# Attention blocks of a two-layer decoder trunk: 1/z, V and value transfers on other DMA queues, one down-projection look-ahead

## The chip, the core and the metric

The kernel runs on one core of a Trainium2 chip. A core has TensorE (PE, matrix products; its weight loads are listed as PEld), VectorE (DVE), ScalarE (ACT), GpSimd (POOL) and SyncE (SP), which run instruction streams of their own and meet at semaphores. A DMA is issued by SP, ACT or POOL and carried out by 16 shared DMA engines. SP's and ACT's queues appear as hardware queues in the profile, POOL's as a software queue. The metric is the device time of one execution in microseconds (us). Each engine works through its own list in order, so an instruction that waits holds everything behind it on that engine, DMA issues included.

## The reference

The model has one short convolution layer, one attention layer, and a SwiGLU feed-forward after each. Sequence 1024, width 1024, 16 heads of 64, all in float32. What matters here is the attention layer: three dilated branches per head, each a banded causal window, combined by their own log-denominators, which makes one softmax over the union of the branches' keys.

```python
BRANCHES = ((128, 1), (512, 4), (2048, 16))

def dilated_attention_mixer(h, w_qkv, w_out, rel_bias):
    bsz, seq, _ = h.shape
    qkv = (h @ w_qkv).reshape(bsz, seq, 3, N_HEADS, HEAD_DIM)
    q, k, v = qkv[:, :, 0], qkv[:, :, 1], qkv[:, :, 2]
    outs, lses = [], []
    for window, dilation in BRANCHES:
        o, l = dilated_branch(q, k, v, rel_bias, window, dilation)
        outs.append(o)
        lses.append(l)
    alpha = jax.nn.softmax(jnp.stack(lses, axis=0), axis=0)
    o = jnp.sum(alpha[..., None] * jnp.stack(outs, axis=0), axis=0)
    return o.reshape(bsz, seq, D_MODEL).astype(h.dtype) @ w_out

def swiglu(h, w_gate, w_up, w_down):
    return (jax.nn.silu(h @ w_gate) * (h @ w_up)) @ w_down
```

## The kernel before

Activations are kept with features on the 128 partitions and the 1024 positions along a row, in eight tiles `X[0..7]`. Matrix products split each operand into a high and a low part and use three matmuls for each product (L370 to L372, L561 to L563, L1501 to L1503); the splits are made by ACT (the high part, L142) and DVE (the low part, L143). Weights arrive through `load_raw` (SP, L156) and are split by `ensure`, in one fixed list `ops`; `take(key, ahead)` hands out the next one and makes sure that `ahead` further ones are already split. Buffers of 4 KB per partition come from one pool of 41 pages; a new tile takes a page over and waits for its last readers.

The schedule is written by hand: generators yield at points where other work may go between, and the order in which the Python code runs is the order of each engine's list.

The stages, in order: convolution mixer; feed-forward 0 with its last down-projection loop (`feed_forward`: one tile `n` of eight after another, each with `take(("d", 0, n))` and two 512-wide products); the Q/K phase (`qk.mix()`, Q and K of the first six head pairs); attention; feed-forward 1. After the last of feed-forward 0's down weights, the list `ops` goes on with the Q/K weights, so that looking ahead in the last down tiles splits Q/K weights early.

Attention is a loop over 16 heads, `slot(n, ...)`, here called block n, with one more at the end. Head pair p is n // 2, its half a is n % 2. A block interleaves on PE: the scores of head n (`scores`, L1556 and L1557), the value products of head n-1 (`values`, L1629), and dense filling work (V tiles by `value_tiles`, Q/K projections of the last two pairs, the output projection of the first half). What else a block issues:

- `load_bias(n+1)` (SP, L1452 and L1453) and `load_kq(n+1)` (SP, L1530 to L1534): bias, keys `ka`, queries `qa` and their low part `ql` of the next head. They come back from DRAM, where the projections left them. `classes(n+1)` copies the keys in another order into `kca` (ACT, L1540).
- `softmax(n)`: POOL takes the maximum over partitions (`mb`, L1610), DVE subtracts (L1618), ACT takes the exponential (L1619). The value products need the results.
- `load_values(p)`: the values of pair p into the single buffer `vx`, six DMAs per pair (ACT, L1518 and L1520), from `vdram`, where `value_tiles` stored them (ACT, L1510, four DMAs for each of eight tiles). Up to block `LAG` = 13 it is issued in the odd blocks, after the loads of head n+1; the last pair's comes at the end of block 14's first half. The last value product of the pair before must have read `vx`.
- `values` ends with ACT's copies of the products and the denominators to `o` and `z` (L1652, L1653).
- `finish(p)`: the denominators of a pair go to DRAM and back in another shape (POOL, L1661 and L1664), DVE takes 1/z (L1666), POOL stores it (L1667), and SP loads it spread over 128 partitions (L1669): 64 rows hold one head's 1024 numbers, the other 64 the other head's. One block later `attended()` multiplies (DVE, L1716) and POOL stores the result to `odram` (L1717). The last pair takes another way; its second half is spread by two POOL loads of 64 rows (L1707).
- Before block 12, `load_attended` (SP, L1804) fetches the first four results from `odram`; they are split (`w_hi<-oin`) for the output projection of the first half.

In the compiled order the DMAs of SP and ACT use eight completion semaphores in turn, those of POOL another eight.

Of the kernel before, what the change touches and what calls it, by code (L numbers as in the profile page):

```python
# [17 lines left out]
S = 1024  # L18
# [31 lines left out]
LAG = 13  # L50
# [48 lines left out]
def trunk(ctx: ExitStack, tc: tile.TileContext, x, gains_in, cwi, ck, cwo, wqkv, wo, relb,  # L99
          wg, wu, wd, oneh, ident, out):  # L100
    nc = tc.nc
# [69 lines left out]
    def take(key, ahead=1):  # L171
        i = op_state[1]
        assert ops[i][0] == key, (ops[i][0], key)
        ensure(i + ahead)
        op_state[1] += 1
        return made.pop(i)
# [210 lines left out]
    def both(w, ks, acts):  # L387
        banks = two_banks()
        run(product(w, ks, acts, banks))
        return banks  # L390
# [99 lines left out]
    def add_to_x(n, banks):  # L490
        for (c0, c1), b in banks.items():
            nc.vector.tensor_tensor(out=X[n][:, c0:c1], in0=X[n][:, c0:c1], in1=b[:, :c1 - c0], op=ALU.add)  # L492
# [733 lines left out]
    class Swiglu(Strassen):  # L1226
# [111 lines left out]
        def feed_forward(self, stats, last_step, after, final=None):  # L1338
            prep = []

            def start(n):
                if n == 0:
                    last_step()
                    for m in (6, 7):
                        combos[self.key, 1](m)
                    ensure(self.at(3, 1))
                if n == self.key + 1:
                    next(stats)
                    combos[self.key, 2](6)
                    ensure(self.at(0, 6))  # L1350
                elif n == self.key + 2:
                    run(stats)
                    prep.append(self.second_half())
                    next(prep[0])
                    nc.scalar.activation(scratch, eps, AF.Silu)
                    ensure(self.at(1, 6))
                elif n == 4:
                    ensure(self.at(1, 7))
                elif n in (5, 7, 8, 10, 12):
                    next(prep[0], None)  # L1360
                if n in (8, 24):
                    self.ahead = 3 if n == 8 else 2

            self.run(start)
            key = ("d", self.key)
            if final:
                final(key, self.plain, self.hid)
                return
            for n in range(KT):
                add_to_x(n, both(take(key + (n,)), self.plain, self.hid))  # L1370
                after(n)

    def by_columns(key, ks, acts, pieces, each, between, wide=4, ahead=1, added=lambda i, n: None):
# [92 lines left out]
    def attention(norm, qk):  # L1466
# [5 lines left out]
        vx = scope["pool"].tile([128, 16, 192], F32, name="vx", tag="vx", bufs=1)  # L1472
# [17 lines left out]
        def value_tiles(g, j):  # L1490

            if j == 0:
                wv[:] = [take(("v", g, i), 1) for i in range(2)]
            v = page("v")
            for b4 in range(4):
                t = 4 * j + b4
                b = bank()[:, :256]
                for k in range(KT):
                    (hi, lo), (whi, wlo) = qk.h[j][k], wv[k // 4]
                    a, c = slice(b4 * 128, b4 * 128 + 128), slice(k % 4 * 256, k % 4 * 256 + 256)  # L1500
                    nc.tensor.matmul(b, hi[:, a], whi[:, c], start=k == 0, stop=False)  # L1501
                    nc.tensor.matmul(b, hi[:, a], wlo[:, c], start=False, stop=False)
                    nc.tensor.matmul(b, lo[:, a], whi[:, c], start=False, stop=k == KT - 1)  # L1503
                    if k % 2:
                        yield
                nc.scalar.activation(v[:, b4 * 256:b4 * 256 + 256], b, AF.Identity, scale=norm.r[:, t:t + 1])
                yield
            vd = vdram[g]
            for r in range(4):
                nc.scalar.dma_start(bass.AP(vd.tensor, vd.offset + (512 * j + r) * 256,  # L1510
                                          [[16 * 256, 32], [4 * 256, 4], [1, 256]]), v[32 * r:32 * r + 32])

        def load_values(p):
            src = vdram[p // 2]
            for a in range(2):
                off = src.offset + p % 2 * 128 + a * 64
                dims = slice(128 * a, 128 * a + 64)
                nc.scalar.dma_start(vx[:, 0:8, dims], bass.AP(src.tensor, off, [[256, 128], [128 * 256, 8], [1, 64]]))  # L1518
                for h in range(2):
                    nc.scalar.dma_start(vx[:, 8 + 4 * h:12 + 4 * h, dims],  # L1520
                                        bass.AP(src.tensor, off + 512 * 256 * h, [[1024, 128], [256, 4], [1, 64]]))

        def load_kq(n):
# [132 lines left out]
        def finish(p):  # L1656

            o, z = OZ.pop(p)
            if p < NPAIR - 1:
                zd, rd = zdram[p]  # L1660
                nc.gpsimd.dma_start(zd, z[0:65:64])  # L1661
                yield
                zc = scope["pool"].tile([128, 16], F32, name="zc", tag="zc", bufs=2)
                nc.gpsimd.dma_start(zc, bass.AP(zd.tensor, zd.offset, [[16, 128], [1, 16]]))  # L1664
                yield
                nc.vector.reciprocal(zc, zc)  # L1666
                nc.gpsimd.dma_start(bass.AP(rd.tensor, rd.offset, [[16, 128], [1, 16]]), zc)  # L1667
                yield
                nc.sync.dma_start(z, bass.AP(rd.tensor, rd.offset, [[S, 2], [0, 64], [1, S]]))  # L1669
                yield  # L1670
                put_off.append((p, o, z))
                return

            zd, rd = zdram[p]
            wide = lambda t: bass.AP(t.tensor, t.offset, [[HALF, 2], [1, HALF]])
            thin = lambda t: bass.AP(t.tensor, t.offset, [[8, 128], [1, 8]])
            nc.gpsimd.dma_start(wide(zd), z[0:65:64, HALF:])
            zc = scope["pool"].tile([128, 8], F32, name="zl", tag="zl", bufs=1)
            nc.gpsimd.dma_start(zc, thin(zd))
            acts[p] = page("o_hi", F32R), page("o_lo", F32R)  # L1680

            def scaled(c0, c1):
                q = slice(c0, c1)
                nc.vector.tensor_tensor(out=o[:, q], in0=o[:, q], in1=z[:, q], op=ALU.mult)

            def parts(h):
                split(o[:, half(h)], [t[:, half(h)] for t in acts[p]])

            for c in (0, 256):
                nc.vector.reciprocal(z[:, c:c + 256], z[:, c:c + 256])  # L1690
                scaled(c, c + 256)
                if c:
                    parts(0)
                    nc.scalar.activation(scratch, eps, AF.Sqrt)
                yield

            def rest():
                scaled(HALF, S)
                parts(1)

            last_part.append(rest)
            yield
            ensure(ahead_ao + KT - AO_WIDE)
            nc.vector.reciprocal(zc, zc)
            nc.gpsimd.dma_start(thin(rd), zc)
            for a in range(2):
                nc.gpsimd.dma_start(z[64 * a:64 * a + 64, HALF:],  # L1707
                                    bass.AP(rd.tensor, rd.offset + a * HALF, [[0, 64], [1, HALF]]))
            ensure(ahead_ao + KT - AO_WIDE + 4)
            yield  # L1710
# [11 lines left out]
        def slot(n, dense, ndense, late=0, hook=iter(())):  # L1722
# [5 lines left out]
            p, a = divmod(n, 2)  # L1728
            if n < H:
                new = dict(bias=bias.pop(n))  # L1730
                sc = scores(p, a, new)
            else:
                sc = iter(())
            if n + 1 < H:
                bias[n + 1] = load_bias(n + 1)
                load_kq(n + 1)
# [14 lines left out]
                extra = finish(p - 1)  # L1751
            used = 0
            if lagged:
                if a:
                    load_values(p)
                for i in range(8):
                    next(sc, None)
                    if n or i % 2:
                        other(1)
                        used += 1  # L1760
                    if i in (0, 3):
                        next(extra, None)
                run(sc)
            else:
                if a == 0 and not late:
                    other(1)
                    used += 1
                for i in range(8):
                    next(sc, None)
                    next(pv, None)  # L1770
                    next(pv, None)
                    if i >= late and i % 2 == 0:
                        other(1)
                        used += 1
                run(sc)
                run(pv)
                if a == 0:
                    extra = finish(p - 1)
                if a == 0 and n < H:
                    load_values(p)  # L1780
# [279 lines left out]
```

## Time and profile before

| | us |
|---|---|
| median of 3 runs | 2200.01 (2198.01 to 2201.2) |
| profiled execution | 2200.59 |
| its span, first to last instruction | 2198.8 |
| mean granted TensorE clock | 0.986 |
| PE busy | 2121.2 |
| DVE busy | 1746.1 |
| ACT busy | 1006.7 |
| POOL busy | 228.5 |

The profile is one execution. Its head gives busy time per engine; a view by stretches gives the same for any window, with the clock that was granted to TensorE and the share of time in which the 16 DMA engines were busy. The view of waits has rows "who waited <- for whom: us in all, times, longest". The chain of waits follows back from the last instruction what released what. A timeline row is start, duration, engine, line, operation, tiles, and in brackets the idle time before it with its releaser. "SPq" and "ACTq" are the DMA issues of an engine.

### The profile page before, as it was taken

The numbers are of one execution on the slowest core, as the hardware profiler recorded it, in microseconds if no ns is written. First come the engines' busy times: TensorE is split into PE (matmuls) and PEld (weight loads), VectorE is DVE, ScalarE is ACT, GpSimd is POOL, SyncE is SP. The second block draws the span as 40 slices with busy tenths as digits, with TensorE's granted clock in tenths as the row PEclk, the third lists the DMA queues.
The fourth block names the chain that finished last, engine by engine and source line by source line (L and its number), as shares of the span: only waits on it lengthen the run. The fifth ranks groups of instructions, "written<-read, shape, count | busy, mean of one in ns | idle before, by whom it ended". The sixth has DMA issues, their size and how long they took to land. (4 is left out here: it accounts for less than half of the span.)

```text
span 2198.8 us, 30951 instructions
## 1 busy us (share of the span) xinstructions
PE 2121.2 (96%) x11086; PEld 1817.0 (83%) x11086; DVE 1746.1 (79%) x3272; ACT 1006.7 (46%) x1848; POOL 228.5 (10%) x324
## 2 busy tenths in 40 slices
PE   9999999999999999999998888799999999999998
PEld 7788888888888888877898778688888888888887
DVE  8898669988888888779856467567998888888886
ACT  7333336444444554355443443434644444446335
POOL 1000000101010010001312122121010100101000
PEclk9999999999999999999999999899999999999999
DMA  7222643233333584334674656755223333267532
GB/s 216 88 90 68 229 144 86 87 106 111 106 111 106 185 235 158 108 125 139 235 190 118 167 166 169 195 157 180 68 105 106 108 108 106 104 210 213 174 91 77
DMA packets 146215, 304.90 MB, mean 139 GB/s; under 512 B 48732, under 2 KB 59212, under 8 KB 146062
## 3 DMA queue, kind: packets, MB, share of 16 engines
q1 hardware_dynamic: 74862, 197.22, 29.4%
q0 software_dynamic: 25424, 78.42, 11.1%
q10 hardware_dynamic: 45776, 27.29, 4.3%
q8 instruction: 88, 1.44, 0.3%
q14 instruction: 65, 0.53, 0.1%
HBM read 212.48 MB, written 83.05 MB: 134 GB/s over the span
## 5 line engine op out<-in xcount | busy, mean ns | idle before, releaser
L563 PE MATMUL bank<-b,w 128*128 128x512 f32 x1952 | 760.9, 390 | 6.1 <-DVE w L143 6.0
L561 PE MATMUL bank<-b,w 128*128 128x512 f32 x1952 | 762.7, 391 | 1.5 <-ACT w L142 1.1
L562 PE MATMUL bank<-b,w 128*128 128x512 f32 x1952 | 760.4, 390 | 0.6 <-DVE b L872 0.6
L563 PEld LDWEIGHTS bank<-b,w 128*128 128x128 f32 x1952 | 366.4, 188 | 87.5 <-DVE w L143 10.8
L561 PEld LDWEIGHTS bank<-b,w 128*128 128x128 f32 x1952 | 366.6, 188 | 78.0 <-ACT w L142 1.7
L562 PEld LDWEIGHTS bank<-b,w 128*128 128x128 f32 x1952 | 366.6, 188 | 76.1 <-DVE b L872 1.4
L142 ACT ACTIVATE w<-combo 128x512 fp32r<-128x512 f32 (+2 forms) x488 | 249.1, 540 | 231.2 <-DVE combo L190 214.1
L143 DVE TENSOR_TENSOR w<-combo,w 128x512 fp32r<-128x512 f32 (+2 forms) x488 | 276.3, 579 | 38.1 <-ACT w L142 37.4
L567 ACT ACTIVATE part<-bank 128x512 f32<-128x512 f32 x186 | 110.7, 596 | 388.6 <-PE bank L563 386.7
L143 DVE TENSOR_TENSOR w<-raw,w 128x512 fp32r<-128x512 f32 (+2 forms) x342 | 188.5, 572 | 46.9 <-ACT w L142 46.9
L571 DVE TENSOR_TENSOR part<-part,bank 128x256 f32<-128x256 f32 (+1 forms) x366 | 170.6, 495 | 31.2 <-PE bank L563 16.7
L142 ACT ACTIVATE w<-raw 128x512 fp32r<-128x512 f32 (+2 forms) x342 | 167.1, 530 | 52.3 <-PE bank L563 12.2
L370 PE MATMUL bank<-w_hi,w 128*128 128x512 f32 (+1 forms) x400 | 153.9, 385 | 18.6 <-ACT w_hi L142 13.7
L371 PE MATMUL bank<-w_lo,w 128*128 128x512 f32 (+1 forms) x400 | 150.2, 375 | 1.6 <-DVE w_lo L143 1.6
L372 PE MATMUL bank<-w_hi,w 128*128 128x512 f32 (+1 forms) x400 | 149.9, 375 | 1.1 <-DVE w L143 1.1
L791 DVE TENSOR_TENSOR x<-x,bank 128x512 f32<-128x512 f32 x136 | 92.5, 680 | 29.3 <-PE bank L563 29.3
L190 DVE TENSOR_TENSOR combo<-raw 128x512 f32<-128x512 f32 (+1 forms) x172 | 111.2, 646 | 0.0
L492 DVE TENSOR_TENSOR x<-x,bank 128x512 f32<-128x512 f32 (+1 forms) x104 | 66.2, 642 | 54.9 <-PE bank L372 54.3
L370 PEld LDWEIGHTS bank<-w_hi,w 128*128 128x128 f32 x400 | 75.9, 190 | 32.4 <-ACT w_hi L142 14.1
L371 PEld LDWEIGHTS bank<-w_lo,w 128*128 128x128 f32 x400 | 76.0, 190 | 15.6 <-DVE w_lo L143 2.9
L372 PEld LDWEIGHTS bank<-w_hi,w 128*128 128x128 f32 x400 | 75.8, 190 | 15.4 <-DVE w L143 2.1
L554 DVE TENSOR_TENSOR b<-hin,b 128x512 fp32r<-128x512 f32 x126 | 79.4, 683 | 9.4 <-ACT b L553 9.3
(245 smaller groups left out, 3491.8 us busy)
## 6 DMA issues: line engine op xcount, KB each, us to landing
hin<-part SPq DMA_DIRECT2D x126, 256.0 KB
raw<-in_ffn_w_gate SPq DMA_DIRECT2D x44, 512.0 KB
raw<-in_ffn_w_up SPq DMA_DIRECT2D x44, 512.0 KB
part<-sum POOLq DMA_DIRECT2D x72, 256.0 KB, 2.3
raw<-in_ffn_w_down SPq DMA_DIRECT2D x48, 384.0 KB
raw<-in_attn_w_qkv SPq DMA_DIRECT2D x27, 512.0 KB
raw<-in_conv_w_in SPq DMA_DIRECT2D x24, 512.0 KB
part<-part POOLq DMA_DIRECT2D x36, 256.0 KB, 2.4
```

Of the source, the lines that this page charges most:

```text
L142: nc.scalar.activation(hi, src, AF.Copy)
L143: eng.tensor_tensor(out=lo, in0=src, in1=hi, op=ALU.subtract)
L190: eng.tensor_tensor(out=c, in0=a, in1=b, op=op)
L370: nc.tensor.matmul(b, whi[:, a], ahi[:, s], start=first, stop=False)
L371: nc.tensor.matmul(b, whi[:, a], alo[:, s], start=False, stop=False)
L372: nc.tensor.matmul(b, wlo[:, a], ahi[:, s], start=False, stop=last)
L561: nc.tensor.matmul(b, hi[:, a], bhi, start=start and k == 0, stop=False, skip_group_check=True)
L562: nc.tensor.matmul(b, hi[:, a], blo, start=False, stop=False, skip_group_check=True)
L563: nc.tensor.matmul(b, lo[:, a], bhi, start=False, stop=k == n - 1, skip_group_check=True)
L567: nc.scalar.activation(t, b, AF.Copy)
L571: nc.vector.tensor_tensor(out=t, in0=t, in1=b, op=ALU.add)
L791: nc.vector.tensor_tensor(out=X[n][:, half(h)], in0=X[n][:, half(h)], in1=b, op=ALU.add)
```

## The change

Four things, in one diff:

1. In the last down tiles of feed-forward 0 (n of 4 to 7), the look-ahead over the list of weights is two instead of one.
2. The stores of V tiles to `vdram` are issued by POOL instead of ACT.
3. `load_values` is issued by SP instead of ACT, and in the odd blocks up to 13 it stands at the front of the block, ahead of the loads of bias, keys and queries of head n+1. The last pair's stays where it was.
4. 1/z is loaded by POOL in two loads of 64 rows each, instead of one load by SP whose pattern is led by a dimension of two.

```diff
             for n in range(KT):
-                add_to_x(n, both(take(key + (n,)), self.plain, self.hid))
+                add_to_x(n, both(take(key + (n,), 2 if n > 3 else 1), self.plain, self.hid))
                 after(n)
...
             for r in range(4):
-                nc.scalar.dma_start(bass.AP(vd.tensor, vd.offset + (512 * j + r) * 256,
+                nc.gpsimd.dma_start(bass.AP(vd.tensor, vd.offset + (512 * j + r) * 256,
                                           [[16 * 256, 32], [4 * 256, 4], [1, 256]]), v[32 * r:32 * r + 32])
...
-                nc.scalar.dma_start(vx[:, 0:8, dims], bass.AP(src.tensor, off, [[256, 128], [128 * 256, 8], [1, 64]]))
+                nc.sync.dma_start(vx[:, 0:8, dims], bass.AP(src.tensor, off, [[256, 128], [128 * 256, 8], [1, 64]]))
                 for h in range(2):
-                    nc.scalar.dma_start(vx[:, 8 + 4 * h:12 + 4 * h, dims],
+                    nc.sync.dma_start(vx[:, 8 + 4 * h:12 + 4 * h, dims],
                                         bass.AP(src.tensor, off + 512 * 256 * h, [[1024, 128], [256, 4], [1, 64]]))
...
                 yield
-                nc.sync.dma_start(z, bass.AP(rd.tensor, rd.offset, [[S, 2], [0, 64], [1, S]]))
+                for a in range(2):
+                    nc.gpsimd.dma_start(z[64 * a:64 * a + 64], bass.AP(rd.tensor, rd.offset + a * S, [[0, 64], [1, S]]))
                 yield
                 put_off.append((p, o, z))
...
                 sc = iter(())
+            if n <= LAG and n % 2:
+                load_values(p)
             if n + 1 < H:
                 bias[n + 1] = load_bias(n + 1)
                 load_kq(n + 1)
...
             if lagged:
-                if a:
-                    load_values(p)
                 for i in range(8):
```

## The prediction

> **What bounds the kernel now.** I read the page's head, then the table by stretches, to see where TensorE (PE) is not busy.
>
> ```profile
> span 2198.8 us, 30951 instructions
> PE 2121.2 (96%) x11086; PEld 1817.0 (83%) x11086; DVE 1746.1 (79%) x3272; ACT 1006.7 (46%) x1848; POOL 228.5 (10%) x324
> ...
> 1100.00:1500.00 400.00, 342.01 (x2412) 318.17 (x2411) 244.26 (x434) 164.26 (x237) 76.90 (x62) 0.93 0.63 166
> ```
>
> The columns of a stretch are its length, then busy time of PE, weight loads, DVE, ACT and POOL, then granted clock, DMA share and GB/s. PE is the bound everywhere, but of its 77.6 idle us (2198.8 - 2121.2) 58.0 lie between 1100 and 1500 us (400 - 342.01), the attention blocks. The clock is also 0.93 there. No other engine is above 62% in that stretch, so the idle time is waiting, not another bound.
>
> Next, the seven long stops. Each stretch begins where PE ran dry and ends where the clock is back at 1.00.
>
> ```profile
> 1165.10:1176.30 11.20, 5.16 (x23) 4.84 (x23) 3.97 (x5) 6.86 (x11) 0.50 (x1) 0.70 0.57 141
> 1212.90:1220.70 7.80, 4.55 (x26) 4.52 (x26) 1.51 (x4) 5.67 (x8) 0.00 (x0) 0.78 0.96 221
> 1257.50:1268.50 11.00, 4.52 (x18) 3.88 (x17) 5.06 (x5) 4.52 (x5) 1.63 (x3) 0.69 0.97 238
> 1308.40:1319.70 11.30, 5.97 (x22) 5.02 (x21) 4.80 (x6) 8.42 (x12) 0.55 (x1) 0.70 0.67 191
> 1354.60:1364.10 9.50, 4.10 (x19) 3.77 (x19) 5.89 (x9) 6.49 (x10) 0.56 (x1) 0.64 0.88 220
> 1397.80:1415.30 17.50, 4.34 (x15) 3.46 (x15) 4.76 (x7) 9.54 (x13) 0.00 (x0) 0.61 0.78 230
> 1458.90:1469.90 11.00, 5.68 (x20) 4.79 (x20) 5.93 (x9) 6.71 (x9) 1.63 (x3) 0.69 0.59 174
> ...
> 1315.19 0.63 PE L370 MATMUL bank<-b,w_hi 128*128 128x512 f32 x1
> 1315.62 0.63 PE L371 MATMUL bank<-b,w_hi 128*128 128x512 f32 x1
> ...
> 1321.16 0.40 PE L370 MATMUL bank<-b,w_hi 128*128 128x512 f32 x1
> 1321.39 0.40 PE L371 MATMUL bank<-b,w_hi 128*128 128x512 f32 x1
> ```
>
> A stop costs twice. PE is idle, and the work after it runs at the low clock: starts 0.43 us apart (1315.19 to 1315.62) against 0.23 (1321.16 to 1321.39), so about 45% of that busy time is lost. Rows two to seven: length 68.10, busy 29.17, idle 38.9, lost to the clock 0.45 x 29.17 = 13.1; together 52.0 us.
>
> What is waited for? The chain of waits, and the stretches just before those stops:
>
> ```profile
> 1194.31 16.16 DMA ka<-kq
> 1211.20 3.82 DMA bias<-tables
> 1296.86 17.48 DMA ql<-kq
> 1339.72 17.75 DMA ka<-kq
> 1364.40 7.09 DMA vx<-vdram
> 1433.99 1.70 DMA rdram<-zc
> 1435.83 14.98 DMA z<-rdram
> ...
> 1202.00:1208.00 6.00, 6.00 (x55) 6.00 (x54) 3.87 (x8) 0.00 (x0) 2.90 (x1) 1.00 0.13 51
> 1252.00:1256.00 4.00, 4.00 (x32) 3.74 (x30) 2.41 (x4) 0.00 (x0) 2.33 (x1) 1.00 0.13 52
> ...
> SPq L1669 <- DMA rdram<-zc: 87.0, 7, 22.0
> ACT kca L1540 <- DMA ka<-kq: 53.4, 4, 14.6
> ```
>
> The spread of 1/z (L1669) takes about 15 us for 512 KB. In its tail, here for the first two of the seven, the DMA share is 0.13, two engines of sixteen, at 51 GB/s. The next head's keys and queries queue behind it (16 to 18 us to land), ACT waits for them in order (53.4 us, 14.6 at most), its exponentials come late, and PE runs dry. SP is also held 87.0 us before the spread may start, with those loads behind it.
>
> **The change part by part.**
>
> *1/z in two loads of 64 rows from GpSimd.* The profile has such a pair in the last head pair, half as wide:
>
> ```profile
> z<-rdram POOLq DMA_DIRECT2D x2, 128.0 KB, 2.8
> kq<-kq_hi POOLq DMA_DIRECT2D x32, 256.0 KB, 4.0
> ...
> L1707 POOL DMA_DIRECT2D z<-rdram x2: 522/534/546, 1517.4 to 1517.9; - x2
> ```
>
> Each 64-row load of 128 KB landed in 2.8 us and GpSimd took 534 ns (median) to issue one. For 256 KB I take 4.0 us, the nearest row of that size; bounds are 2.8 and today's 15. At 4.0 the jam is gone, and with it the stops of rows two to five, and of seven together with the value loads below. Row six shrinks rather than vanishes:
>
> ```profile
> 1395.14 1.23 DVE L1618 TENSOR_TENSOR lf<-lf,mb 128x1024 f32<-128x1024 f32 x1 [0.29 <-POOL mb L1610]
> ...
> 1406.10 1.04 ACT L1619 ACTIVATE lf<-lf 128x1024 f32<-128x1024 f32 x1
> ...
> 1409.45 1.04 ACT L142 ACTIVATE w_hi<-oin 128x1024 fp32r<-128x1024 f32 x1
> ```
>
> Without the wait for keys the exponentials start when DVE's difference is there (1396.4 instead of 1406.1), so the split that PE needs moves forward 9.7 us and some 5 of that row's 15 stay. Recovered: 52.0 - 5 = 47.0. The price on GpSimd: it waits for the store of 1/z to land (1.7) and issues twice (1.1), with key stores, the next column maximum (mb) and the next z store behind it; 7 x 2.8 = 19.6 us if nothing hides it, and nothing if mb waits for DVE anyway. I take nothing.
>
> [...]
>
> *V stores by GpSimd, value loads by SP.* ACT loses both:
>
> ```profile
> L1510 ACTq DMA_DIRECT2D vdram<-v x32: 557/612/1510, 1101.9 to 1412.8; - x32
> ...
> 1169.38 2.00 ACT L142 ACTIVATE w_hi<-raw 128x1024 fp32r<-128x1024 f32 x2 [1.72 <-issue]
> ...
> 1461.12 2.10 ACT L1540 ACTIVATE kca<-ka 128x512 fp32r<-128x512 f32 x2 [9.79 <-DMA vx<-vdram]
> ```
>
> The three columns of a tile's row are its shortest, median and longest issue in ns. The weights that end the first stop were split behind four V stores of 0.61; ACT's idle 1.7 us there comes back. Row seven is ACT held 9.79 us by its value loads, already counted. Two short PE waits for values (2.9 us) and the last exponential's lateness behind z (1.7) go as well:
>
> ```profile
> PE bank L1629 <- DMA vx<-vdram: 2.9, 2, 1.6
> ...
> 1491.02 1.16 PE L1629 MATMUL bank<-lf,vx 128*128 128x128 f32 x8 [1.72 <-ACT lf L1619]
> 973.32 0.50 PE L563 MATMUL bank<-b,w 128*128 128x512 f32 x1 [1.53 <-DVE w L143]
> ```
>
> That is 4.6 us. The last row is the gap at the start of the Q/K phase, where PE waits for a weight's low part: *weights two ahead* makes that part one tile earlier, under a down tile's matmuls, so 1.5 us. If the extra split were not covered it would cost its DVE time once, below 1 us.
>
> [...]
>
> *What the new order costs.* In an odd block n, SP now issues six value loads first, and these wait for the last matmul that reads the old values, at the end of block n-1. Bias and keys of block n+1 stand behind them. For block 3:
>
> ```profile
> 1174.92 0.59 ACT L1652 ACTIVATE z<-bank 64x512 f32<-64x512 f32 x1 [2.33 <-PE bank L1629]
> ...
> 1191.08 1.06 ACT L1619 ACTIVATE lf<-lf 128x1024 f32<-128x1024 f32 x1 [3.08 <-DVE lf L1618]
> ```
>
> From 1174.9: six value issues and two of bias and two of keys at 0.61 each, keys issued by +6.1. Landing takes 3.8 (the bias row) to 7.1 us (the value row), the copy for classes (kca) 2.1: done at +12.0 to +15.3. ACT's exponentials begin at +16.2, so it fits with 0.9 to 4.2 us left. Only odd blocks 3 to 13 have it, six. Bounds per block: 0, or 9.6 if keys land as late as today (17.5). I take 2, near the fitting end, because eight completion semaphores in turn make SP wait for the eighth load before. That is 12 us; range value 6 each, 36.
>
> **Sum:** 47.0 + 1.7 + 4.6 + 1.5 = 54.8 off, 12 on: 42.8 off. The profiled execution took 2200.59 (its span and 1.8 around it): 2157.8. It is 0.6 above the runs' median 2200.01, so I say 2157.
>
> **The rivals.**
>
> *A, slower: keys late in odd blocks.* Place: SP behind the value loads of blocks 3 to 13. If keys land 17.5 us after their issue, kca ends at +25.7, exponentials 9.5 late, and the clock adds 0.45 x 5 = 2.3: six times 11.8 is 71 against 54.8 recovered, 2217. It decides from 9.1 us a block, keys landing some 15 us after issue. For it: values now sit in front of keys in one queue. Against: 16 to 18 us appear only behind the spread; values alone took 7.1.
>
> *B, the spread stays slow on GpSimd.* Then the two engines stay jammed, and only 1.7 + 2.9 + 1.5 and row seven's 5.3 + 2.6 come back: 14.0 - 12 = 2, 2199, no change. For it: half the bytes per load, same source row. Against: 2.8 us of the last pair.
>
> *C, GpSimd becomes the gate.* The 19.6 above, and V stores in front of mb, 6 x 4 x 0.53 = 13: 33 us, 2190. For it: GpSimd works in order and PE needs each mb. Against:
>
> ```profile
> POOL mb L1610 <- DVE m L1607: 91.5, 8, 24.4
> ```
>
> GpSimd stood idle 91.5 us before eight of the sixteen reductions, waiting for DVE.
>
> **How the numbers follow.** About 0.2% (4.4 us) is what a measurement of this kernel can tell from no change. Forecast 0.80; C's full price 0.08; A 0.05; B 0.04; better than 2140, 0.03. The low end is no new wait and row six gone (17 us): 2140. The high end is 6 us in each odd block (24 more) and a little of C: 2184. Faster is forecast, C and better, 0.91; same is B, 0.04; slower is A, 0.05.
>
> **What would show it.** Right: z landing in about 4 us, no stretch with share 0.13, keys landing under 8 us, PE idle in attention down from 58 to some 15 to 25 us with the clock near 0.98, ACT's wait for keys below 15 us. Wrong: keys still landing in 16 us (B), ACT's kca waiting for keys in the blocks after odd value loads (A), DVE waiting for mb well beyond the 3 us of a reduction (C). The gap at 973 closing shows the two-ahead step alone.

## The result and the profile after

The changed kernel is faster: 2147.05 us as the median of 4 runs (2143.22 to 2153.36) against 2199.31 us for the kernel before in the same session, a ratio of 0.9765 with a 95% interval of 0.9738 to 0.9791. Repeated in a later session (run e9 below) it took 2151.07, ratio 0.9777 (0.9763 to 0.9791). The gain by medians is 52.3 and 48.0 us; 43 were forecast, and 2157 us lay 10 above the first median.

The profiled execution took 2144.75 us, its span 2142.9. The page's head, and the row by stretches for the attention blocks (length; busy PE, weight loads, DVE, ACT, POOL; clock, DMA share, GB/s):

```profile
span 2142.9 us, 30996 instructions
PE 2109.1 (98%) x11086; PEld 1808.6 (84%) x11086; DVE 1747.6 (82%) x3272; ACT 1008.1 (47%) x1848; POOL 255.8 (12%) x370
...
1100.00:1500.00 400.00, 384.43 (x2652) 354.63 (x2651) 289.81 (x504) 197.00 (x290) 111.13 (x118) 0.98 0.71 191
```

PE's idle time fell from 77.6 to 33.8 us (2142.9 - 2109.1), and its busy time for the same 11086 instructions by 12.1, because more of them ran at the full clock: 43.8 + 12.1 is the whole 55.9 of the span. In the stretch, idle went from 58.0 to 15.6 us and the clock from 0.93 to 0.98. The same stretch does not hold the same work in both kernels, but both kernels run the same matmuls in the same order, so one can be counted off in both traces: the kernel before starts the matmul that the changed kernel starts at 1110 us 1.0 us later, the one at 1466 us 55.9 us later, and it is still 55.9 behind at the end. All but 1.0 us of the gain therefore lies where the prediction looked for it.

What is left in the changed kernel, in order: the issue row of the spread (count, KB each, median us to landing), the view of waits (us in all, times, longest), and TensorE's timeline where it stood still:

```profile
z<-rdram POOLq DMA_DIRECT2D x14, 256.0 KB, 4.8
...
ACT kca L1540 <- DMA ka<-kq: 28.0, 8, 10.8
DVE lf L1618 <- POOL mb L1610: 26.9, 11, 3.5
SPq L1518 <- PE bank L1629: 68.3, 8, 16.6
...
977.13 0.50 PE L561 MATMUL bank<-b,w 128*128 128x512 f32 x1 [0.63 <-ACT w L142]
1163.42 0.58 PE L1501 MATMUL bank<-w_hi,b 128*128 128x256 f32 x1 [3.54 <-ACT w_hi L142]
1270.44 0.38 PE L1556 MATMUL bank<-qa,ka 128*128 128x256 f32 x1 [1.28 <-ACT o L1653]
1366.93 0.79 PE L370 MATMUL bank<-w_hi,w 128*128 128x512 f32 x1 [3.26 <-ACT w_hi L142]
```

The spread lands in 4.8 us instead of 15. Of the seven long stops, two remain in shorter form, at 1163 and 1367, and both wait for weights or attention results that ACT splits behind its exponentials. A third, of 2.36 us before 1350.95, is shown in the last section. SP is still held, now by the value loads that wait for PE (68.3 us), where before it was held by the stored 1/z (87.0).

### The profile page after: what moved, and what is told of

It reads as the page before. It is cut to its first block, busy times and chain, and to the rows that moved or that the text cites. A ratio compares the mean times of both kernels' runs of the same rounds, so it can differ in the third digit from the quotient of the medians.

```text
span 2142.9 us, 30996 instructions
## 1 busy us (share of the span) xinstructions
PE 2109.1 (98%) x11086; PEld 1808.6 (84%) x11086; DVE 1747.6 (82%) x3272; ACT 1008.1 (47%) x1848; POOL 255.8 (12%) x370
```

## The experiments

Eleven runs (e9 is the changed kernel itself), in three sessions on three chips, each session with runs of the kernel before (medians 2198.78, 2198.00 and 2199.10). "Gain" below is the before's median less the kernel's.

### Which part of the z edit works: engines or queue

**e1: the kernel before with the z edit alone.**

```diff
-                nc.sync.dma_start(z, bass.AP(rd.tensor, rd.offset, [[S, 2], [0, 64], [1, S]]))
+                for a in range(2):
+                    nc.gpsimd.dma_start(z[64 * a:64 * a + 64], bass.AP(rd.tensor, rd.offset + a * S, [[0, 64], [1, S]]))
```

> Only the spread of 1/z is changed: two 64-row loads by GpSimd; V stores, value loads and the look-ahead stay as before. Theory E (the old pattern ran on two DMA engines): the stops two to five vanish, row seven stays partly because ACT still issues the value loads; some 35 to 42 us off, about 2160, and no stretch with DMA share 0.13. Theory Q (what counts is that SP is no longer held 87 us before it may issue the spread): the same 2160, with ka landing under 8 us. Theory A (ACT's queue relief carries the gain): at most 10 us off, 2190.

**e2: the same two loads, but still issued by SP** (`nc.sync` in the added line).

> Two 64-row loads as in the change, but still issued by SP at the old place, nothing else changed. Theory E: nearly the gain of the GpSimd version, 30 to 42 us off, 2158 to 2170, since the tail on two engines is gone though SP is still held. Theory Q: little, under 10 us off, above 2190.

**e3: the old single load, pattern unchanged, issued by POOL.**

```diff
-                nc.sync.dma_start(z, bass.AP(rd.tensor, rd.offset, [[S, 2], [0, 64], [1, S]]))
+                nc.gpsimd.dma_start(z, bass.AP(rd.tensor, rd.offset, [[S, 2], [0, 64], [1, S]]))
```

> One load with the old pattern led by a dimension of two, issued by GpSimd instead of SP, nothing else changed. Theory E: the load takes some 15 us, the two engines stay jammed and keys that land after it stay late; 2190 to 2200. Theory Q: SP is free, so 25 to 42 us off, 2158 to 2175.

**e4: the change without its z edit** (parts 1 to 3 of the change).

> The change without its 1/z part: V stores by GpSimd, value loads by SP in front of the block, weights two ahead; 1/z as before. Theory E: 0 to 15 us off, 2185 to 2200, with all of the stops two to five still there. Theory A: 35 us off or more, 2165.

| | us | ratio, 95% | gain |
|---|---|---|---|
| e1, two loads, POOL | 2149.86 | 0.9781, 0.9766 to 0.9795 | 48.9 |
| e2, two loads, SP | 2152.80 | 0.9789, 0.9771 to 0.9808 | 46.0 |
| e3, one old load, POOL | 2183.37 | 0.9938, 0.9919 to 0.9957 | 15.4 |
| e4, all but z | 2187.27 | 0.9950, 0.9935 to 0.9965 | 11.5 |

The issue row of the spread in e1, then in e2 that row and SP's own waits:

```profile
z<-rdram POOLq DMA_DIRECT2D x14, 256.0 KB, 5.2
...
z<-rdram SPq DMA_DIRECT2D x14, 256.0 KB, 3.6
...
SPq L1670 <- DMA rdram<-zc: 83.5, 7, 19.0
```

A stretch of the changed kernel in which the two loads of one pair (issued at 1353.4 and 1353.9) move almost all the data:

```profile
1355.00:1356.50 1.50, 1.33 (x12) 1.20 (x11) 1.50 (x5) 1.50 (x3) 0.00 (x0) 1.00 1.00 288
```

In e3 the issue row, a stretch in the tail of one of the loads, VectorE's row when that load has landed, and TensorE's row after it:

```profile
z<-rdram POOLq DMA_DIRECT2D x7, 512.0 KB, 15.0
...
1384.00:1388.00 4.00, 0.29 (x3) 0.10 (x1) 0.00 (x0) 0.00 (x0) 0.00 (x0) 0.93 0.13 52
...
1388.33 1.23 DVE L1716 TENSOR_TENSOR o<-o,z 128x1024 f32<-128x1024 f32 x1 [10.25 <-DMA z<-rdram]
...
1395.44 0.79 PE L370 MATMUL bank<-w_hi,w 128*128 128x512 f32 x1 [11.15 <-ACT w_hi L142]
```

And in e4 the wait for keys, with TensorE's longest stop:

```profile
ACT kca L1540 <- DMA ka<-kq: 99.4, 13, 19.0
...
1399.80 0.80 PE L370 MATMUL bank<-w_hi,w 128*128 128x512 f32 x1 [17.12 <-ACT w_hi L142]
```

This separates two things that the edit does at once. In e2 SP is held for 83.5 us, about as long as before (87.0), and yet 46.0 us are gained: with the new pattern the hold costs nothing that these times show (e1 and e2 overlap in their intervals). In e3 SP is free of that wait, but the load still takes 15.0 us with a tail at a share of 0.13, and only 15.4 us are gained. In the stretch shown every engine stands still (0.29 us of PE in 4.00): VectorE waits 10.25 us for the spread itself, with the next differences for the exponentials behind that product. So the pattern carries most of the gain; freeing SP is worth something only while the pattern is slow, and the 15.4 us are a net figure, since VectorE's waits for the spread grew from 18.1 us before to 37.1 in e3.

The edit also makes two loads out of one. The old load's tail kept two engines' worth busy (0.13 of 16 is 2.1). If each of the two did no more, their share could be 0.26 at most (twice 0.13, an estimate); the stretch of the changed kernel has 1.00 at 288 GB/s. The number of engines has therefore changed, not only the number of loads.

e3 has its tail at 0.13 and 52 GB/s from POOL, as the kernel before has at 0.13 and 51 GB/s from SP: the other queue alone changed nothing in it. Two loads to partition halves took the spread from 15 us to 3.6 from SP (e2) and 5.2 from POOL (e1).

Against the expectations: e1 and e2 gained more than theory E gave them (up to 42 us). e3 lies between both of its ranges. e4 lies in its range for theory E, but not with all of the stops two to five still there: row two's is gone and row four's is 1.4 us at the longest.

The four kernels also show that the parts do not add: 48.9 + 11.5 is 60.4, and the whole change gave 48.0 to 52.3. In e1 and in e4 alike the stops of rows two, four and seven are gone or down to 1.9 us, so the other three parts relieve stops that the z edit removes anyway. How much of the difference is instead the cost of the new SP order, below, is not separated, since e4 has that order too.

### The other parts, each taken back from the changed kernel

**e5: the value loads back on ACT at their old place.**

```diff
-                nc.sync.dma_start(vx[:, 0:8, dims], bass.AP(src.tensor, off, [[256, 128], [128 * 256, 8], [1, 64]]))
+                nc.scalar.dma_start(vx[:, 0:8, dims], bass.AP(src.tensor, off, [[256, 128], [128 * 256, 8], [1, 64]]))
                 for h in range(2):
-                    nc.sync.dma_start(vx[:, 8 + 4 * h:12 + 4 * h, dims],
+                    nc.scalar.dma_start(vx[:, 8 + 4 * h:12 + 4 * h, dims],
...
-            if n <= LAG and n % 2:
-                load_values(p)
...
             if lagged:
+                if a:
+                    load_values(p)
```

> The change but with value loads left on ACT at their old place. If the value loads on SP are worth what the prediction's last stop and the two value waits say (7.9 + 2.9), 2155 to 2159. If the two-engine spread had been holding ACT's value loads too, so that the last stop goes with it anyway, 2145 to 2150 and kca in the last head no longer 10 us late.

**e6: the value loads on SP, but behind the loads of head n+1** (the last two hunks of e5 alone).

> The change, value loads by SP, but behind the loads of head n+1 as before (inside the block, not at its front). If keys waiting behind values cost 2 us in each of six odd blocks, as predicted, this is 12 us faster than the change: 2135. If nothing is lost there because keys have slack, within 3 us of it, or slower by up to 10 because SP issues values a block's keys later and value products wait: 2147 to 2157.

**e7: the V stores back on ACT** (`nc.scalar` at L1510).

> The change but with V stores left on ACT. The prediction gives them 1.7 us at the first stop: 2149. If GpSimd as the gate costs something (up to 13 us for 24 V stores ahead of a reduction), this is faster than the change: 2134 to 2144.

**e8: the look-ahead back to one** (`take(key + (n,))` at L1370).

> The change without the look-ahead of two in the last down tiles. The gap of 1.5 us at the start of the Q/K phase should be back and nothing else: 1 to 2 us slower than the change, 2148 to 2149, which may not be told from none by the times; the trace should show the gap.

**e9: the changed kernel once more, beside e10 and e11.**

> The changed kernel as it is, once more, beside a kernel with the old value-load order (e11, with one more edit) on one chip. Theory (value loads at the front of SP cost about 6 us): 2147 again, 5 to 7 us above 2141. Rival (the 6 us was a difference between chips or runs, since the intervals 0.9738 to 0.9791 and 0.9725 to 0.9753 overlap): 2141 to 2143.

| | us | ratio, 95% | gain |
|---|---|---|---|
| e5, values on ACT, old place | 2141.34 | 0.9742, 0.9728 to 0.9755 | 56.7 |
| e6, values on SP, old place | 2140.71 | 0.9739, 0.9725 to 0.9753 | 57.3 |
| e7, V stores on ACT | 2153.60 | 0.9800, 0.9786 to 0.9814 | 44.4 |
| e8, look-ahead one | 2148.86 | 0.9779, 0.9765 to 0.9793 | 49.1 |
| the change, first session | 2147.05 | 0.9765, 0.9738 to 0.9791 | 52.3 |
| e9, the change again | 2151.07 | 0.9777, 0.9763 to 0.9791 | 48.0 |

Against the expectations: e5 is faster than both of its ranges and e7 slower than both; e6 lies between its two, and e9 is 10.4 us above e6, where 5 to 7 were expected of the order and 0 to 2 of a mere difference between chips.

*Value loads.* Both e5 and e6 are faster than the change, and the repeat e9 does not overlap with either: the place at the front of SP's block costs 0.0026 to 0.0038 of the time, 6 to 8 us. Which of the two queues issues them makes no difference that the times show (e5 and e6 agree within 1 us in their medians). SP's timeline of the changed kernel shows how, around block 7:

```profile
1233.45 0.43 SPq L1518 DMA_DIRECT2D vx<-vdram  x1
1233.93 1.26 SPq L1520 DMA_DIRECT2D vx<-vdram  x2
1242.80 0.38 SPq L1518 DMA_DIRECT2D vx<-vdram  x1
1243.22 1.76 SPq L1520 DMA_DIRECT2D vx<-vdram  x2
1245.08 2.38 SPq L1452 DMA_DIRECT2D bias<-tables  x1
...
1248.27 0.49 SPq L1530 DMA_DIRECT2D ka<-kq  x1
```

The same keys in e6, then ACT's copy of them and its next row of exponentials in e6:

```profile
1240.31 0.47 SPq L1530 DMA_DIRECT2D ka<-kq  x1
...
1250.86 2.15 ACT L1540 ACTIVATE kca<-ka 128x512 fp32r<-128x512 f32 x2
...
1260.73 1.06 ACT L1619 ACTIVATE lf<-lf 128x1024 f32<-128x1024 f32 x1 [7.72 <-DVE lf L1618]
```

and ACT's two rows in the changed kernel:

```profile
1254.65 2.16 ACT L1540 ACTIVATE kca<-ka 128x512 fp32r<-128x512 f32 x2 [4.35 <-DMA ka<-kq]
...
1265.06 1.06 ACT L1619 ACTIVATE lf<-lf 128x1024 f32<-128x1024 f32 x1 [8.25 <-DVE lf L1618]
```

The six loads come in two halves. The first three (1233.45) replace the half of `vx` that the earlier head of the pair read, so they go out 9 us ahead of the others; only the last three (1242.80) wait for the block's last product. Keys are issued at 1248.27 instead of 1240.31, ACT waits 4.35 us for them, and the exponentials start 4.3 us later than in e6. PE stops for 1.28 us at 1270.44, where e6 has no stop above 0.8 us between 1165 and 1306.

Counted by matmuls, e6 gains 4.3 us on the changed kernel between 1214 and 1275, around this block, 2.6 between 1348 and 1352, at the stop of 2.36 us, and 0.6 us at most between any other neighbouring points compared: two places, not six. The places depend on what else is queued: e10 below has the same order, loses nothing at these two and 5.0 us between 1362 and 1372 instead.

*V stores.* e7 is 5 to 8 us slower than the change; its interval overlaps with that of e9 a little, so the times leave the size loose. Better separated are e5 (z, V stores and look-ahead) and e1 (z alone): 0.0039, or 8.6 us for the two parts. The third and fourth of ACT's first four V stores in e7, then two rows of ACT and two of TensorE:

```profile
1105.06 0.56 ACTq L1510 DMA_DIRECT2D vdram<-v  x1
1108.65 0.56 ACTq L1510 DMA_DIRECT2D vdram<-v  x1
1109.26 0.84 ACT L1506 ACTIVATE v<-bank,r 128x256 f32<-128x256 f32 x2 [7.80 <-DMA vdram<-v]
...
1116.05 2.00 ACT L142 ACTIVATE w_hi<-raw 128x1024 fp32r<-128x1024 f32 x2 [3.07 <-DMA ka<-kq]
...
1134.19 0.55 PE L1556 MATMUL bank<-qa,ka 128*128 128x256 f32 x1 [2.33 <-DVE lf L1567]
1169.92 0.58 PE L1501 MATMUL bank<-w_hi,b 128*128 128x256 f32 x1 [5.46 <-ACT w_hi L142]
```

Counting matmuls settles it: the one at 1169.92 is the one at 1163.42 in the changed kernel, and up to 1110 us the two traces are 0.6 us apart, so 5.9 us are lost between. The kernel before, e1, e2 and e3, all with V stores on ACT, fall back by 4.5 to 6.0 us there; e4 to e6 and e8 to e10, with V stores on POOL, by 0.3 at most. The stop at 1169.92 is 5.46 against 3.54 us: 1.9 us, the four issues before the weight split. The stop at 1134.19 is 2.33 against 0.89, another 1.4. The rest is a stop of 0.88 us at 1118.42, for a weight whose split starts at 1116.05 instead of 1112.29, and a stretch at low clock.

ACT is held before that split too, 7.80 us in one piece. The row names a store that landed late, but the issues themselves were held: the third of the four goes out at 1105.06 and the fourth at 1108.65, when the completion semaphores that they take over come free. By the trace these belonged to a bias load and a query load that SP had issued at 1100.23 and 1102.11. In the trace of the kernel before, the DMAs of SP and ACT name the same eight semaphores, those of POOL eight others, and ACT's stores wait there in the same way: the third goes out at 1106.11, when the semaphore of a bias load that SP issued at 1100.66 is complete (1106.08), the fourth at 1109.52, after that of a query load of 1102.55 (1109.49).

*Look-ahead.* e8 and the change cannot be told apart (0.9779 against 0.9765 and 0.9777). TensorE's row in e8 shows the old gap again:

```profile
973.65 0.50 PE L563 MATMUL bank<-b,w 128*128 128x512 f32 x1 [1.52 <-DVE w L143]
```

In the changed kernel this gap is gone, and PE waits 0.63 us for ACT a little later, at 977.13. Counted by matmuls, e8, e1 and the kernel before all fall back by 0.7 us between 970 and 980. So 0.7 us are shown, and no more.

### The queue of z in the full change, and a faster kernel

**e10: the change, with the two z loads issued by SP** (`nc.sync` at L1670).

> The change with the two 64-row loads of 1/z issued by SP instead of GpSimd, all else as changed. Theory (the number of engines that the pattern takes carries the gain; the queue is second): SP is held by the wait for the stored 1/z, 1.7 us at a time and more, behind value loads that also hold it, so keys come a little later: 2148 to 2156, z landing about 4 us. Rival (GpSimd's queue matters as soon as value loads are on SP too): 2165 or more, the stops back in some odd blocks.

It took 2147.93 us, ratio 0.9768 (0.9752 to 0.9785), the same as e9 on the same chip. So the rival, that the queue matters as soon as value loads share it, falls. Its waits and its longest stop:

```profile
ACT kca L1540 <- DMA ka<-kq: 46.7, 11, 12.2
...
1366.52 0.79 PE L370 MATMUL bank<-w_hi,w 128*128 128x512 f32 x1 [8.24 <-ACT w_hi L142]
```

ACT waits longer for keys than in the changed kernel (46.7 against 28.0 us), and one stop at 1366 has grown from 3.26 to 8.24, but the total is no worse. ACT's waiting time is therefore a poor marker of what PE loses.

**e11: e6 with the next V weights split earlier.**

```diff
                     if k % 2:
                         yield
+                if j and b4 == 1:
+                    ensure(op_state[1] + 1)
                 nc.scalar.activation(v[:, b4 * 256:b4 * 256 + 256], b, AF.Identity, scale=norm.r[:, t:t + 1])
```

> The change with the value loads on SP behind head n+1's loads (as e6) and with one more edit: the first V weights of each next group are split while the second tile of the group before runs (an ensure of one further weight there). Theory (what is left of the stops is weights split behind the exponentials): the 3.5 us stop at 1160 us goes, with 2 to 3 us of its low clock: 2134 to 2138 against e6's 2140.7. Rival (the page pool is full, so that the early split waits for a page or moves another wait there): 2140 to 2146.

It took 2136.86 us, ratio 0.9717 (0.9703 to 0.9730): a gain of 62.2, and the fastest of the study. Against e9 on the same chip it is 14.2 us faster, and the intervals are apart. Against e6, on another chip, it is 0.0022 faster with intervals that overlap, so the edit's own 5 us are not separated by the times. The stretch of the attention blocks and TensorE's one remaining long stop in e11, and that stop in e6:

```profile
1100.00:1500.00 400.00, 389.33 (x2698) 359.00 (x2697) 296.32 (x517) 200.09 (x297) 113.54 (x120) 0.99 0.71 194
...
1356.35 0.80 PE L370 MATMUL bank<-w_hi,w 128*128 128x512 f32 x1 [5.33 <-ACT w_hi L142]
...
1359.92 0.49 PE L370 MATMUL bank<-w_hi,w 128*128 128x512 f32 x1 [3.20 <-ACT w_hi L142]
```

The stop at 1160 is gone, and idle time in the stretch is 10.7 us against 12.3 in e6 and 15.6 in the changed kernel. Counted by matmuls, e11 has gained 5.4 us on e6 by 1214 and gives 2.4 of them back by the end, most of it at the stop at 1356, which grew from 3.20 to 5.33. What remains is the split of the attended results before the output projection; moving that was not tried.

## Why the prediction was right, and where its sizes were off

The sign, the mechanism and the range held. Step by step:

- **The stops come from the spread on two engines, and cost idle time and clock together: right in the main.** e3 keeps the pattern and the 0.13 stretches, and gains 15.4 of the 48.9 us; in e2, with the pattern gone and SP's hold kept, the stops of rows two to five and seven are down to 1.9 us. What the prediction left out is that VectorE waits for the slow spread too (18.1 us before, 37.1 in e3). In the changed kernel 43.8 us of idle and 12.1 of clock came back.
- **z lands in 4.0 us; 47.0 recovered there: right.** 4.8 us measured with POOL, 3.6 with SP; 48.9 us gained by e1, 46.0 by e2. No price on GpSimd was taken, and none shows: e1 and e2, and e9 and e10, cannot be told apart. The 4.6 us that the prediction put down to moving the value loads (two waits for values and the last exponential) came with the z edit: with values back on ACT (e5), PE waits 0.8 us for them in all.

```profile
PE bank L1629 <- DMA vx<-vdram: 0.8, 1, 0.8
```

- **Value loads by SP instead of ACT, with the 2.9 us of waits put down to it: no difference shown.** e5 and e6 differ in the issuing engine alone and agree within 1 us in their medians (2141.34 and 2140.71). The 2.9 us went all the same, since the jam behind the spread had caused them: e1, with its value loads still on ACT, has no wait of PE for values.
- **V stores off ACT, 1.7: too small.** The 1.7 at the one stop measured 1.9, but the part is worth 4.5 to 6.0 us by matmuls and 5 to 8 by e7's times. The step counted issue time at one stop and left out the two stops before it, at 1118 and 1134. ACT's issues, held for SP's loads, stand before both; how much of the two stops they cause is not shown.
- **The new SP order, 2 us in each of six blocks, 12: right in sign, too large, and not in each block.** e6, against the change and e9, puts it at 6 to 8 us, lost at two places. The step's premise that six value loads wait for the last product was wrong: in the block shown three do, the other three go out earlier. That alone moves little, since keys still go out 5.5 us after the waiting three start, against the 6.1 forecast; in the other blocks the count of matmuls shows no loss.
- **Look-ahead, 1.5: too large.** 0.7 us are shown.
- **The sum, 42.8 against 48.0 to 52.3:** the missing 5 to 9.5 us are about the V stores' 3 to 6 more and the order's 4 to 6 less, with the z part, values included, 2.7 us below the 51.6 forecast for it and the look-ahead 0.8 below. That errors of both signs left the total only 5 to 10 us off is in part luck. Two of the working's figures are off in the last digit (29.17 for 29.16, 9.6 for 9.5), which changes nothing.
- **Row six keeps some 5 us: near.** The stop at 1366.93 is what is left of it, 3.26 us idle and a stretch at low clock:

```profile
1366.90:1376.00 9.10, 8.32 (x29) 6.64 (x30) 6.08 (x7) 6.69 (x10) 3.33 (x6) 0.62 0.49 119
```

  The clock is at 0.50 from 1366.93 to 1373.76; at the prediction's 45% that costs some 3 us of the busy time there, so that about 6 us are left (an estimate).
- **Rival A (keys late, 2217)** has its mechanism in block 7 above, but 6 to 8 us in all, and not 71: keys in front of which values stand are issued 8 us late there, and the copy of them starts 6.4 us after their issue, where the rival had them land after 17.5. **Rival B (spread stays slow on POOL)** falls with e1; e3 shows what it would have looked like. **Rival C (POOL becomes the gate)** falls: DVE's waits for the column maximum are 3.5 us at the longest, about the reduction itself (3.2 us), though POOL's own wait for the stored 1/z is up to 7.1 us and not 1.7:

```profile
POOL z L1670 <- DMA rdram<-zc: 21.5, 5, 7.1
```

- **"ACT's wait for keys below 15 us": missed.** It was 28.0 in the profiled run and 13.3 in the slower e9; e10 shows why it is no good sign. PE idle of 15 to 25 us (15.6) and the clock of 0.98 were met, and so were keys under 8 us: from block 1 on, where ACT waits for them, their copy starts 7.1 us after the issue at the latest. Stretches of a low share remain in which no spread moves data (0.10 from 1350.90, in the last section), so a share of 0.13 by itself is no sign either.

## What to carry to other kernels

Look at the DMA share before a stop, not only at who waits: here 0.13 (of 16 engines 2.1), with transfers queued behind, was the tail of one load, and two loads with a pattern led by 64 rows instead of two cured it from either queue (15 us became 5.2 from POOL, 3.6 from SP). Count matmuls to compare two traces of the same work: that sized parts which the times could not. Before a DMA issue is moved to the front of another queue, read which of its parts wait, and for what; here the moved value loads gave back 6 to 8 us, and leaving them behind the keys was faster. Look for what a DMA issue waits for as well: stores on ACT were held by SP's loads (7.80 us of ACT in e7). After the big stall is gone, the next ones here are small splits behind a row of exponentials; asking for one of them a tile earlier took its stop away and lengthened the next by 2.1 us.

## What was not expected of the hardware

In the changed kernel's trace, how long TensorE stood still did not alone decide whether the clock fell; where the stop lay counted too. The matmul after the stop of 1.28 us at 1270.44 (its row is shown with the result), and a stop of 2.36 us with the stretch behind it:

```profile
1271.67 0.79 PE L370 MATMUL bank<-b,w_hi 128*128 128x512 f32 x1 [0.48 <-ACT o L1653]
...
1350.95 0.38 PE L1556 MATMUL bank<-qa,ka 128*128 128x256 f32 x1 [2.36 <-ACT v L1506]
...
1350.90:1354.50 3.60, 3.55 (x29) 3.55 (x30) 3.48 (x9) 2.73 (x5) 1.03 (x2) 1.00 0.10 37
```

After the shorter stop the clock falls to 0.50, after the longer one it stays at 1.00. In the attention blocks of this trace it falls at 1162.13, 1271.36 and 1366.93 and comes back after 6.83, 3.41 and 6.83 us. The shortest of these low stretches is 3.413 us, and the three falls lie 32 and 28 such steps apart. Stretches along these steps, two around each stop:

```profile
1267.95:1271.36 3.41, 1.82 (x10) 1.07 (x8) 2.45 (x7) 3.35 (x7) 1.13 (x2) 1.00 0.97 253
1271.36:1274.77 3.41, 3.10 (x9) 2.67 (x10) 3.34 (x8) 0.25 (x1) 0.00 (x0) 0.50 0.26 102
...
1346.45:1349.86 3.41, 2.14 (x19) 1.93 (x17) 3.41 (x7) 2.89 (x4) 0.58 (x1) 1.00 1.05 278
1349.86:1353.28 3.42, 2.33 (x19) 2.33 (x20) 3.34 (x9) 3.35 (x8) 0.00 (x0) 1.00 0.34 133
```

The short stop lies whole in one step, which stood idle for 1.59 us in all (3.41 - 1.82), and the next step ran at 0.50. The long stop is cut in two, 1.27 and 1.09 us. In the thirteen traces, between 1000 and 1550 us, no step at full clock with less than 1.4 us idle was followed by one at 0.50, and every one with more than 1.8 us was; between the two both occur. In the trace of the kernel before the steps that were followed had 2.32 to 3.41 us idle, the others 1.57 at most; in that of the changed kernel 1.59, 2.24 and 3.26, the others 1.27 at most.
